# A layer norm in two scalar_tensor_tensor steps, and a down product with its contraction outside

## The chip, the cores and the metric

One core of one Trainium2 chip runs the program. The metric is the device time of one execution in microseconds (us). A core has a matrix engine (TensorE, PE in the rows; PEld are its weight loads), a vector engine (VectorE, DVE), an activation engine (ScalarE, ACT), a general engine (GpSimd, POOL) and SyncE (SP), which here only issues transfers. Each engine runs its own instructions in the order in which the program lists them for it; semaphores order the engines against each other.

## What is computed

One layer of a streaming encoder over 2048 tokens of width 1024. A mixer comes first; its output goes into a layer norm, then into a mixture of 32 experts of which each token uses two, then into a second layer norm and a gated embedding:

```
x   = layer_norm(ALPHA * x + mixer(x), ln1_g, ln1_b)
ffn = moe(x)                       # per token: two experts, weighted by e_w
                                   # expert: (silu(x @ w_eg) * (x @ w_eu)) @ w_ed
x   = layer_norm(ALPHA * x + ffn, ln2_g, ln2_b)
out = x + sigmoid(x @ w_pg + b_pg) * rms_norm(p @ w_pp, ple_g)

def layer_norm(x, g, b):
    mu  = mean(x);  var = mean((x - mu) ** 2)
    return (x - mu) * rsqrt(var + EPS) * g + b
```

## The kernel before

Only the expert phase and the last phase matter here.

**The expert phase** (class Experts, about 900 to 1686 us of the trace) walks a fixed list of items. An item is the gate ("g"), up ("u") or down ("d") product of one block of 128 gathered rows; there are 33 blocks of one expert and 7 pair blocks of two experts, 64 rows each. Weights of single experts come in two units per matrix, are loaded as f32 (eraw), and are split into a high part on ScalarE and a low part on VectorE (ew), so that three matrix products stand for one. Weights of an expert that is seen only in a pair block come as one whole tile of 2 MB and are loaded straight into a weight slot, with no split (L1704). There are seven weight slots, handed on first in, first out: a slot is freed after the item that uses its unit last, and the next unit of the list takes it. The transfer into a reused slot waits, on SyncE's queue, for the last product that reads the old contents.

**A down product** (Block.down) makes 1024 output columns in two halves of 512. For each half it takes one of two PSUM banks with the tag "yo", runs four contraction steps of three products (12 matmuls), and copies the bank to y on ScalarE (L1473). Steps 0 and 1 read the first weight unit (d, 0), steps 2 and 3 the second (d, 1). Between the halves it hands control back to the list (yield), which puts in transposes and weight splits of other items. With this order the first unit is read by the matmuls 1 to 6 and 13 to 18 of 24.

**The last phase** (class Final, 16 tiles of 128 tokens, written t) gathers two expert rows per token (L1810) and the residual (xn), forms the weighted sum (ln, L1826 to L1828, with the row sum as accum_out), calls layer_norm with that sum as total (L901 to L915), transposes the result (tr, L1486, split by L46 on ScalarE and L47 on VectorE), multiplies by w_pg (gate, 48 matmuls, L56 to L58, evicted by L1840), and closes the tile: sigmoid (L1849), product with the embedding (L1850), sum (L1851), store. The embedding's own norm takes a square on ScalarE (L1945), a power and a product with the gain on GpSimd (L1953, L1954); the list places these behind the power L905 of the layer norm three tiles on.

In layer_norm with total given, VectorE makes mean and minus mean (L901, L902), ScalarE squares with accumulation (L903, its elementwise output thrown away into "spare"), VectorE makes the variance (L904), GpSimd takes the power -0.5 (L905), VectorE makes minus mean times that (L906), ScalarE normalises in place (L907), and VectorE multiplies by g and adds b in halves of 512 columns (L914, L915). The scheduler may put instructions of other steps between these. `after(k, ctx, insts)` puts the instructions of a block behind each given instruction, on that instruction's own engine only; RS[t], what layer_norm returns, is used for that.

Buffers: the gathered pair yy has five slots, xn three, the output x2 four from tile 4 on, gt (gate result, and scratch of L1945) two.

Of the kernel before, what the change touches and what calls it, by code (L numbers as in the profile page):

```python
# [12 lines left out]
AF = mybir.ActivationFunctionType  # L13
OP = mybir.AluOpType
# [26 lines left out]
def ptile(k, tag, shape):  # L41
    return k.psp.tile(shape, F32, name=tag, tag=tag, bufs=k.pb[tag])
# [74 lines left out]
def drain(g):  # L117
    for _ in g:
        pass
# [769 lines left out]
def layer_norm(k, p, r, g, b, out, total=None, spare=None, keep=False):  # L889


    nc, v = k.nc, k.nc.vector
    m = p.tile([128, 5], F32, name="lnm", bufs=2)
    if total is None:
        st = p.tile([128, 2, 6], F32, name="lnst", bufs=2)
        for i in range(2):
            v.bn_stats(st[:, i], r[:, 512 * i:512 * i + 512])
        v.bn_aggr(m[:, 0:2], st)
        v.tensor_scalar(m[:, 2:3], m[:, 1:2], EPS, None, OP.add)
    else:  # L900
        v.tensor_scalar(m[:, 0:1], total, 1.0 / D, None, OP.mult)  # L901
        v.tensor_scalar(m[:, 4:5], total, -1.0 / D, None, OP.mult)  # L902
        nc.scalar.activation(spare, r, AF.Square, bias=m[:, 4:5], accum_out=m[:, 1:2])  # L903
        v.tensor_scalar(m[:, 2:3], m[:, 1:2], 1.0 / D, EPS, OP.mult, OP.add)  # L904
    rs = nc.gpsimd.tensor_tensor(m[:, 3:4], m[:, 2:3], k.mhalf[:, 0:1], OP.pow)  # L905
    ms = v.scalar_tensor_tensor(m[:, 4:5], m[:, 0:1], -1.0, m[:, 3:4], OP.mult, OP.mult)  # L906
    no = nc.scalar.activation(r, r, AF.Identity, scale=m[:, 3:4], bias=m[:, 4:5])  # L907
    if total is None:
        rg = out if keep else r
        nc.gpsimd.tensor_tensor(rg, r, g, OP.mult)  # L910
        v.tensor_tensor(out, rg, b, OP.add)
        return rs, no, ms
    for sl in (slice(0, 512), slice(512, 1024)):
        v.tensor_tensor(r[:, sl], r[:, sl], g[:, sl], OP.mult)  # L914
        v.tensor_tensor(out[:, sl], r[:, sl], b[:, sl], OP.add)  # L915
    return rs, no, ms


# [488 lines left out]
class Block:  # L1407
# [54 lines left out]
            self.hT = k.mp.tile([128, 2, 4, 128], F32R, name="hT", tag="hT", bufs=2)  # L1462
            self.ht_done = split(k.nc, k, self.hT[:, 0], self.hT[:, 1], ps)

    def down(self, last=False):
        k = self.k
        y = k.mp.tile([128, 1024], F32, name="y", tag="y", bufs=YB)
        for a in range(2):
            ps = ptile(k, "yo", [128, 512])
            for kc in range(4):  # L1470
                self.mm(ps, self.hT, "d", kc, 512 * a, kc == 0, kc == 3)
            sl = slice(512 * a, 512 * a + 512)
            k.nc.scalar.activation(y[:, sl], ps, AF.Copy)  # L1473
            if last:
                k.nc.scalar.dma_start(self.dst[:, sl], y[:, sl])
            if a == 0:
                yield
        if not last:
            k.nc.scalar.dma_start(self.dst, y)
# [126 lines left out]
class Experts:  # L1606
# [105 lines left out]
    def run(self, then, mid):  # L1712

        k, items, need, blocks = self.k, self.items, self.need, self.blocks
        final = min(i for i, (r, n, b) in enumerate(items) if n == items[-1][1])
        last = {u: i for i, us in enumerate(need) for u in us}
# [22 lines left out]
        g = [blocks[xorder[j]].gather() for j in range(NG)][-1]  # L1739
# [14 lines left out]
        for i, (r, n, b) in enumerate(items):  # L1754
            blk = blocks[n, b]
            if i:
                xstep()
            if i == SORTAT:
                order_tokens(k)
            if i == 2:  # L1760
                ctx.close()
            while not all(u in self.ready for u in need[i]):
                self.wstep()
            if r == "d":
                while blk in pend:
                    hstep()
            m = blk.down(i == len(items) - 1) if r == "d" else blk.up(r)
            next(m)
            hstep()
            self.wstep()  # L1770
            if i == len(items) - 1:
                mid()
            drain(m)
            if r == "u":
                pend.append(blk)
                xlive -= 1
            elif r == "d":
                hlive -= not blk.pair
            for u in need[i]:
                if last[u] == i:  # L1780
                    self.free.append(self.slot[u])
            self.wstep()
            if i >= final:
                then(i - final, blk)
# [3 lines left out]
class Final:  # L1788
# [32 lines left out]
    def ln(self, t, p):  # L1821
        k, nc, v = self.k, self.k.nc, self.k.nc.vector
        y0, y1 = self.Y[t]
        xn = self.XN[t]
        tot = p.tile([128, 1], F32, name="tot", bufs=2)
        nc.scalar.activation(xn, xn, AF.Copy, scale=ALPHA)  # L1826
        v.scalar_tensor_tensor(y0, y0, k.ew[:, 0, t:t + 1], xn, OP.mult, OP.add)  # L1827
        v.scalar_tensor_tensor(y0, y1, k.ew[:, 1, t:t + 1], y0, OP.mult, OP.add, accum_out=tot)  # L1828
        self.X2[t] = y1 if t < INPLACE else p.tile([128, 1024], F32, name="x2", tag="x2", bufs=4)
        self.RS[t] = layer_norm(k, p, y0, k.fin[:, 0], k.fin[:, 1], self.X2[t], tot, y1)  # L1830

    def gate(self, t, amidst=lambda: None):
        k, v, W, XT = self.k, self.k.nc.vector, self.W, self.XT[t]
# [293 lines left out]
```

## Time and profile before

| | us |
|---|---|
| median of 3 runs | 1914.25 (1913.67 to 1916.04) |
| the profiled execution, device time | 1919.0 |
| its span, first to last instruction | 1917.1 |
| TensorE busy in the span | 1837.4 (96%) |
| VectorE busy | 1179.4 (62%) |
| ScalarE busy | 907.8 (47%) |
| GpSimd busy | 318.2 (17%) |

The profile is of one execution. Busy shares are means over stages; a matmul row's duration is longer than its distance to the next one, as matmuls are pipelined. What a stage is worth is read from what its engine waited for there. The clock column of the window rows is the granted TensorE clock as a share of 2.4 GHz; 0.50 stands for 1.2 GHz.

### The profile page before, as it was taken

To read this page: it belongs to the slowest core of one execution; us is meant where nothing else is said; L and a number is where in the kernel's file an instruction comes from. 1 tells how busy PE (TensorE), PEld (TensorE's weight loads), DVE (VectorE), ACT (ScalarE), POOL (GpSimd) and SP (SyncE) were. 2 spreads that over 40 slices of the span, in tenths; PEclk is the share of its full clock that TensorE was granted. 3 is DMA by queue.
4 is the path that set the end of the run, shared out by engine and by line. 5 is a ranking of instruction groups with operands and counts; after the bars stand their busy time and mean duration, and the time that the engine had idled before them with its cause. 6 is when DMAs were issued, how large, how long until landed. Compare 5 with 4: busy or idle time off the path is not lost. (4 is left out here: it accounts for less than half of the span.)

```text
span 1917.1 us, 26807 instructions
## 1 busy us (share of the span) xinstructions
PE 1837.4 (96%) x10016; PEld 1458.7 (76%) x10016; DVE 1179.4 (62%) x2184; ACT 907.8 (47%) x1348; POOL 318.2 (17%) x254
## 2 busy tenths in 40 slices
PE   8999999989999999998999999999999999998898
PEld 6877899989988788876867678575857676776777
DVE  8557665787787444447746356154636256578896
ACT  4343434477777322234645255155536265455442
POOL 0000000033433112211000100000000000137543
PEclk9999999999999999999999999999999999998999
DMA  9698844543455533226988996998799876856632
GB/s 282 200 251 236 216 136 144 190 133 127 149 175 164 181 106 120 100 92 238 384 318 297 352 383 233 327 330 320 274 359 381 327 287 263 334 176 232 224 121 78
DMA packets 232325, 442.86 MB, mean 231 GB/s; under 512 B 46400, under 2 KB 88448, under 8 KB 231296
## 3 DMA queue, kind: packets, MB, share of 16 engines
q1 hardware_dynamic: 205760, 357.07, 54.6%
q0 software_dynamic: 12096, 44.05, 6.4%
q10 hardware_dynamic: 14336, 40.01, 5.3%
q8 instruction: 80, 1.31, 0.3%
q14 instruction: 53, 0.43, 0.1%
HBM read 355.61 MB, written 85.46 MB: 230 GB/s over the span
## 5 line engine op out<-in xcount | busy, mean ns | idle before, releaser
L1371 DVE TENSOR_TENSOR ew<-eraw,ew 128x2048 fp32r<-128x2048 f32 x133 | 302.7, 2291 | 196.3 <-ACT ew L1369 194.9
L1438 PE MATMUL mm<-ew,xt 128*128 128x512 f32 x1584 | 378.0, 394 | 0.0
L1438 PEld LDWEIGHTS mm<-ew,xt 128*128 128x128 f32 x1584 | 295.0, 189 | 65.8 <-issue 5.7
L1369 ACT ACTIVATE ew<-eraw 128x2048 fp32r<-128x2048 f32 x133 | 252.8, 1913 | 78.7 <-PE mm L1438 23.0
L1438 PE MATMUL yo<-ew,hT 128*128 128x512 f32 x792 | 187.8, 393 | 0.1
L56 PE MATMUL mm<-wsp,xsp 128*128 128x512 f32 (+1 forms) x512 | 178.0, 348 | 7.9 <-ACT wsp L46 6.3
L1438 PEld LDWEIGHTS yo<-ew,hT 128*128 128x128 f32 x792 | 147.1, 188 | 37.4 <-issue 5.7
L58 PE MATMUL mm<-wsp,xsp 128*128 128x512 f32 (+1 forms) x512 | 173.7, 339 | 0.5 <-DVE xsp L47 0.5
L57 PE MATMUL mm<-wsp,xsp 128*128 128x512 f32 (+1 forms) x512 | 173.8, 339 | 0.0
L1418 POOL DMA_INDIRECT xg<-x1d,idx x40 | 53.7, 1341 | 703.4 <-PE tr L1486 661.3
L56 PEld LDWEIGHTS mm<-wsp,xsp 128*128 128x128 f32 x512 | 97.2, 190 | 26.3 <-issue 7.2
L56 PE MATMUL mm<-ew,xt 128*128 128x512 f32 (+1 forms) x264 | 106.1, 402 | 2.2 <-DVE yy L1840 2.1
L58 PEld LDWEIGHTS mm<-wsp,xsp 128*128 128x128 f32 x512 | 97.1, 190 | 11.5 <-DVE xsp L47 1.0
L1434 PE MATMUL mm<-ew,xt 128*64 128x512 f32 x320 | 96.6, 633 | 9.7 <-DMA ew<-in_w_eg 9.7
L58 PE MATMUL mm<-ew,xt 128*128 128x512 f32 (+1 forms) x264 | 104.6, 397 | 0.8 <-DVE xt L47 0.8
L57 PEld LDWEIGHTS mm<-wsp,xsp 128*128 128x128 f32 x512 | 97.1, 190 | 10.2 <-DVE wsp L47 0.6
L57 PE MATMUL mm<-ew,xt 128*128 128x512 f32 (+1 forms) x264 | 104.5, 396 | 0.0
L56 PE MATMUL mm<-wsp,mt 128*128 128x512 f32 x256 | 104.3, 408 | 0.0
L58 PE MATMUL mm<-wsp,mt 128*128 128x512 f32 x256 | 102.2, 399 | 0.0
L57 PE MATMUL mm<-wsp,mt 128*128 128x512 f32 x256 | 101.7, 397 | 0.0
L1451 DVE TENSOR_TENSOR h<-h,mm 128x512 f32<-128x512 f32 x40 | 27.4, 685 | 111.2 <-PE mm L1438 90.0
L46 ACT ACTIVATE xt<-tr 128x512 fp32r<-128x512 f32 x98 | 53.6, 591 | 84.6 <-PE tr L1486 84.5
(505 smaller groups left out, 3634.5 us busy)
## 6 DMA issues: line engine op xcount, KB each, us to landing
eraw<-in_w_ed SPq DMA_DIRECT2D x44, 1024.0 KB, 9.2
eraw<-in_w_eu SPq DMA_DIRECT2D x43, 1024.0 KB, 8.3
eraw<-in_w_eg SPq DMA_DIRECT2D x42, 1024.0 KB, 10.2
ew<-in_w_eg SPq DMA_DIRECT2D x10, 2048.0 KB, 10.7
ew<-in_w_eu SPq DMA_DIRECT2D x10, 2048.0 KB, 11.3
ew<-in_w_ed SPq DMA_DIRECT2D x10, 2048.0 KB, 13.0
yb<-y ACTq DMA_DIRECT2D x39, 512.0 KB, 5.6
xraw<-in_xt SPq DMA_DIRECT2D x32, 512.0 KB, 4.6
```

Source lines behind the costliest of these rows:

```text
L46: return (nc.scalar.activation(hi, src, AF.Copy), nc.vector.tensor_tensor(lo, src, hi.bitcast(F32), OP.subtract))
L56: nc.tensor.matmul(ps, lhsT=l[0], rhs=r[0], start=start, stop=False)
L57: nc.tensor.matmul(ps, lhsT=l[0], rhs=r[1], start=False, stop=False)
L58: nc.tensor.matmul(ps, lhsT=l[1], rhs=r[0], start=False, stop=stop)
L1369: h = nc.scalar.activation(w[:, 0], raw, AF.Copy)
L1371: return h, eng.tensor_tensor(w[:, 1], raw, w[:, 0].bitcast(F32), OP.subtract)
L1418: return k.nc.gpsimd.indirect_dma_start(out=self.x, out_offset=None, in_=k.x1d, in_offset=bass.IndirectOffsetOnAxis(ap=self.idx, axis=0))
L1434: mm(ps[sl], lhsT=x[:, kc, sl], rhs=whole_get(u, name, kc, a, a + 512), start=start, stop=stop)
L1438: self.last = mm(ps, lhsT=x[:, l, kc], rhs=w[r], start=start and i == 0, stop=stop and i == 2)
L1451: self.h_done = k.nc.vector.tensor_tensor(self.h, self.h, ps, OP.mult)
```

## The change

Two parts. First, layer_norm with total given: one scalar_tensor_tensor on VectorE writes (r - mean) * g to the output tile, needing the mean but not the power; after the power two scalar_tensor_tensor, one for each half of 512 columns, multiply by the power and add b. L906, L907 and the four products and sums of L914 and L915 are gone from this path. "spare" is now the tile xn instead of y1, since y1 may be the output. RS[t] becomes the power and the two halves (before: the power, the normalisation on ScalarE, and L906). The path without total is as before.

Second, Block.down gets an argument free. It is set for a down item of a single-expert block, not the last item, whose two weight units are both used for the last time: 21 of the 33 by the item list (11 of them follow directly on another down item). Such an item takes both "yo" banks at the start, runs the contraction step outside and the two halves inside, hands control back after step 1, and copies both banks at the end. The unit (d, 0) is then read by the matmuls 1 to 12 only.

```diff
@@ layer_norm, total given
         v.tensor_scalar(m[:, 2:3], m[:, 1:2], 1.0 / D, EPS, OP.mult, OP.add)
+        v.scalar_tensor_tensor(out, r, m[:, 0:1], g, OP.subtract, OP.mult)
     rs = nc.gpsimd.tensor_tensor(m[:, 3:4], m[:, 2:3], k.mhalf[:, 0:1], OP.pow)
+    if total is not None:
+        o = [v.scalar_tensor_tensor(out[:, sl], out[:, sl], m[:, 3:4], b[:, sl], OP.mult, OP.add)
+             for sl in (slice(0, 512), slice(512, 1024))]
+        return rs, o[0], o[1]
     ms = v.scalar_tensor_tensor(m[:, 4:5], m[:, 0:1], -1.0, m[:, 3:4], OP.mult, OP.mult)
     no = nc.scalar.activation(r, r, AF.Identity, scale=m[:, 3:4], bias=m[:, 4:5])
...
-    for sl in (slice(0, 512), slice(512, 1024)):
-        v.tensor_tensor(r[:, sl], r[:, sl], g[:, sl], OP.mult)
-        v.tensor_tensor(out[:, sl], r[:, sl], b[:, sl], OP.add)
     return rs, no, ms
@@ Block.down
+        if free and not self.pair:
+            ps = [ptile(k, "yo", [128, 512]) for a in range(2)]
+            for kc in range(4):
+                for a in range(2):
+                    self.mm(ps[a], self.hT, "d", kc, 512 * a, kc == 0, kc == 3)
+                if kc == 1:
+                    yield
+            for a in range(2):
+                k.nc.scalar.activation(y[:, 512 * a:512 * a + 512], ps[a], AF.Copy)
+            k.nc.scalar.dma_start(self.dst, y)
+            return
@@ Experts.run
-            m = blk.down(i == len(items) - 1) if r == "d" else blk.up(r)
+            end = i == len(items) - 1
+            m = blk.down(end, not end and all(last[u] == i for u in need[i])) if r == "d" else blk.up(r)
@@ Final.ln
-        self.RS[t] = layer_norm(k, p, y0, k.fin[:, 0], k.fin[:, 1], self.X2[t], tot, y1)
+        self.RS[t] = layer_norm(k, p, y0, k.fin[:, 0], k.fin[:, 1], self.X2[t], tot, xn)
```

## Rows read from the trace of the kernel before

**Rows 1.** Windows: length, busy PE, PEld, DVE, ACT, POOL, clock, DMA share, GB/s

```profile
1687.00:1711.00 24.00, 20.30 (x80) 15.99 (x81) 14.55 (x31) 12.55 (x15) 9.68 (x10) 0.86 0.51 175
1711.00:1740.00 29.00, 23.02 (x111) 19.14 (x110) 24.25 (x34) 15.07 (x22) 15.15 (x13) 0.91 0.42 142
1740.00:1800.00 60.00, 51.76 (x219) 42.15 (x218) 52.32 (x80) 28.14 (x39) 39.26 (x31) 0.90 0.73 256
1800.00:1850.00 50.00, 46.09 (x211) 36.65 (x210) 46.05 (x67) 22.93 (x32) 23.60 (x17) 1.00 0.47 157
1850.00:1876.40 26.40, 25.94 (x118) 21.61 (x119) 23.28 (x40) 11.91 (x17) 12.41 (x8) 0.94 0.21 80
```

**Rows 2.** TensorE's waits, 1690 to 1917 us: who waited for whom, total, times, longest

```profile
PE tr L1486 <- DVE x L915: 18.5, 8, 6.0
PE mm L56 <- DVE yy L1840: 2.1, 1, 2.1
PE tr L1486 <- DVE yy L915: 1.6, 1, 1.6
```

**Rows 3.** Timeline of one layer norm, tile 7: start, length, engine, line; idle before it

```profile
1772.03 0.58 POOL L905 TENSOR_TENSOR lnm<-lnm,mhalf 128x1 f32<-128x1 f32 x1
1773.09 2.38 POOL L1954 TENSOR_TENSOR pl<-pl,ew 128x1024 f32<-128x1024 f32 x1
1772.64 2.86 DVE L906 SCALAR_TENSOR_TENSOR lnm<-lnm 128x1 f32<-128x1 f32 x1 [0.91 <-issue]
1775.42 1.27 DVE L1828 SCALAR_TENSOR_TENSOR yy<-yy,ew 128x1024 f32<-128x1024 f32 x1
1775.59 1.24 ACT L907 ACTIVATE yy<-yy,lnm 128x1024 f32<-128x1024 f32 x1 [5.92 <-DVE lnm L906]
1776.62 1.27 DVE L1850 SCALAR_TENSOR_TENSOR gt<-pl,sq,gt 128x1024 f32<-128x1024 f32 x1
1777.82 1.28 DVE L914 TENSOR_TENSOR yy<-yy,ew 128x512 f32<-128x512 f32 x2
1779.03 1.28 DVE L915 TENSOR_TENSOR x<-yy,ew 128x512 f32<-128x512 f32 x2
1779.85 1.08 PE L1486 MATMUL tr<-ident,x 128*128 128x128 f32 x4 [3.38 <-DVE x L915]
```

**Rows 4.** VectorE's waits, 1690 to 1917 us

```profile
DVE lnm L906 <- POOL lnm L905: 11.8, 12, 3.0
```

**Rows 5.** ScalarE's waits, 1690 to 1917 us

```profile
ACT gt L1945 <- DMA out<-gt: 24.2, 4, 6.8
```

**Rows 6.** TensorE's waits in the expert phase, 950 to 1680 us

```profile
PE mm L1434 <- DMA ew<-in_w_eg: 9.7, 4, 3.0
```

**Rows 7.** Timeline around one such wait: TensorE, SyncE's queue (SPq), ScalarE's copies

```profile
1059.69 5.60 PE L1438 MATMUL yo<-ew,hT 128*128 128x512 f32 x24
1063.96 0.37 SPq L1704 DMA_DIRECT2D ew<-in_w_eg  x1
1065.13 5.61 PE L1438 MATMUL mm<-ew,xt 128*128 128x512 f32 x24
1065.33 0.60 ACT L1473 ACTIVATE y<-yo 128x512 f32<-128x512 f32 x1 [2.12 <-PE yo L1438]
1075.62 5.34 PE L1434 MATMUL mm<-ew,xt 128*64 128x512 f32 x14 [3.01 <-DMA ew<-in_w_eg]
```

**Rows 8.** The same 14 matmuls behind two others of the four waits, TensorE

```profile
1212.05 5.34 PE L1434 MATMUL mm<-ew,xt 128*64 128x512 f32 x14 [2.11 <-DMA ew<-in_w_eg]
1508.61 3.65 PE L1434 MATMUL mm<-ew,xt 128*64 128x512 f32 x14 [1.83 <-DMA ew<-in_w_eg]
```

**Rows 9.** Windows: behind the first wait, and ahead of the second

```profile
1074.00:1080.00 6.00, 4.38 (x13) 1.36 (x14) 0.00 (x0) 0.00 (x0) 0.00 (x0) 0.72 1.05 402
1200.00:1202.00 2.00, 2.00 (x11) 1.65 (x10) 0.00 (x0) 0.53 (x1) 0.00 (x0) 1.00 0.00 0
```

**Rows 10.** ScalarE's weight split on the page: count, busy, mean ns, idle before

```profile
L1369 ACT ACTIVATE ew<-eraw 128x2048 fp32r<-128x2048 f32 x133 | 252.8, 1913 | 78.7 <-PE mm L1438 23.0
```

More of the change, by code (lines that the diff above doesn't have):

```diff
@@ L904, in layer_norm @@
         v.tensor_scalar(m[:, 2:3], m[:, 1:2], 1.0 / D, EPS, OP.mult, OP.add)
+        v.scalar_tensor_tensor(out, r, m[:, 0:1], g, OP.subtract, OP.mult)
     rs = nc.gpsimd.tensor_tensor(m[:, 3:4], m[:, 2:3], k.mhalf[:, 0:1], OP.pow)
+    if total is not None:
+        o = [v.scalar_tensor_tensor(out[:, sl], out[:, sl], m[:, 3:4], b[:, sl], OP.mult, OP.add)
+             for sl in (slice(0, 512), slice(512, 1024))]
+        return rs, o[0], o[1]
     ms = v.scalar_tensor_tensor(m[:, 4:5], m[:, 0:1], -1.0, m[:, 3:4], OP.mult, OP.mult)
     no = nc.scalar.activation(r, r, AF.Identity, scale=m[:, 3:4], bias=m[:, 4:5])
[L908 to L912, printed above, removed]
-    for sl in (slice(0, 512), slice(512, 1024)):
-        v.tensor_tensor(r[:, sl], r[:, sl], g[:, sl], OP.mult)
-        v.tensor_tensor(out[:, sl], r[:, sl], b[:, sl], OP.add)
+    rg = out if keep else r
+    nc.gpsimd.tensor_tensor(rg, r, g, OP.mult)
+    v.tensor_tensor(out, rg, b, OP.add)
     return rs, no, ms
@@ L1463, in ht, with down @@
             self.ht_done = split(k.nc, k, self.hT[:, 0], self.hT[:, 1], ps)
-    def down(self, last=False):
+    def down(self, last=False, free=False):
         k = self.k
         y = k.mp.tile([128, 1024], F32, name="y", tag="y", bufs=YB)
+        if free and not self.pair:
[9 more added lines that the diff above has]
+            return
         for a in range(2):
```

## Prediction

> **What bounds the kernel now.** I read the page's busy shares first: TensorE is busy 96% of the span, so time can only come from the places where it waits or runs slowly. The view of TensorE's waits, taken by stretch, names them. In the last phase it waits ten times, 18.5 + 2.1 + 1.6 = 22.2 us, nearly all of it for the second product of the layer norm, L915 [rows 2]. In the expert phase it waits four times for one kind of transfer, 9.7 us, longest 3.0 [rows 6]. The window view adds what the waits alone hide: in the stretches of the last phase where they fall, the mean granted clock is 0.86, 0.91, 0.90 and 0.94, and 1.00 where they hardly occur [rows 1]. Time at a mean clock c in a stretch of length L gives L * (1 - c) of lost work: 24 * 0.14 + 29 * 0.09 + 60 * 0.10 + 26.4 * 0.06 = 3.4 + 2.6 + 6.0 + 1.6 = 13.6 us. So the last phase has at most 22.2 + 13.6 = 35.8 us to give.
>
> What bounds it behind that is VectorE: from 1711 to 1876.4 it is busy 24.25 + 52.32 + 46.05 + 23.28 = 145.9 of 165.4 us [rows 1]. The layer norm is late because its steps queue there, not because its data are.
>
> **The layer norm, along its path.** Tile 7 shows the pattern [rows 3]. The power L905 ends at 1772.6. The tiny L906 then takes 2.86 us and ends at 1775.5, together with GpSimd's 1024-column product L1954 (1773.09 to 1775.47): a VectorE instruction with two SBUF inputs stands still while that one runs. Then ScalarE normalises (1775.59 to 1776.83), meanwhile VectorE has begun L1828 and L1850 (to 1777.82), then come two L914 (to 1779.03) and the first L915; TensorE starts its transposes at 1779.85, 3.38 us late.
>
> After the change the first half is one step of 512 columns away from the power. Two L914 issue in 1777.82 to 1779.03, so 512 columns cost 0.60. It has two SBUF inputs as L906 had, and L1954 still comes right behind the power, so I let it wait as L906 did: 1775.5 + 0.6 = 1776.1, and the transposes could start 3.7 us earlier than 1779.85. This wait of 3.38 is gone, and 1776.1 is what the next limit has to beat.
>
> The new first step, 1024 columns with two inputs, costs VectorE what a scalar_tensor_tensor of that size costs: L1828 starts at 1775.42 and L1850 follows at 1776.62, so 1.20 [rows 3]. Per tile: removed 4 * 0.60 = 2.4 and L906, whose own work is one column; added 1.20 + 2 * 0.60 = 2.4. VectorE's work is unchanged. The first step lies beside ScalarE's square and GpSimd's power, where VectorE otherwise waits for L905 (11.8 us in 12 waits [rows 4]); without that cover it would be 1.2 us of path per tile, still less than is removed. ScalarE loses L907, 1.24 us a tile [rows 3]; it is not the bound, so that counts only as latency.
>
> Buffers: the gathered pair is now last read by the first step and the square, ahead of the power, not by L914, so its slot returns by the 1779.0 - 1772.0 = 7 us of [rows 3] earlier, or a little less, and GpSimd's next gathers can start sooner; a gain I don't price. xn is held longer, till the square ends instead of L1827; its loads on SyncE's queue start later, with pl's loads and the stores of gt queued behind. Its price lies between nothing and a few microseconds in the first tiles; I take nothing, since three slots leave two tiles in between.
>
> The sum for this phase, part by part. The waits around tile 1 (1.6 and 2.1): the first goes, one of the second's two microseconds goes, the clock loss of 3.4 goes with them: 6. The longest, 6.0, tile 4: ScalarE's step and the products go (3.0), the rest of the wait and its clock loss stay: 3. The other seven waits, 18.5 - 6.0 = 12.5, and 6.0 + 1.6 of clock: 20.1 at most. That makes 29. But VectorE cannot give all: of its 19.5 idle us in the stretch some 7 will stay (first tiles, data not there yet), which leaves 12.5; with the 6 of tile 1, ahead of that stretch, 18.5. Between 10 (VectorE stays as loosely packed as now, only tile 1 and two waits gain) and 29 I take **18**, since VectorE's busy share in 1800 to 1850 is already 0.92 at full clock [rows 1]: it can be packed so.
>
> By the Trainium skill, Vector Engine (DVE) Microarchitecture Reference, section "Points that are easy to get wrong", a scalar_tensor_tensor with two SBUF sources that are not bf16 runs at half throughput, which speaks against this change. Here L1850 has two such f32 sources and takes the 1.20 us for 1024 columns that two L914 of 512 take [rows 3]; the trace disagrees, and I give the rule a chance of its own below.
>
> **The down product.** All four waits of [rows 6] are for the second whole tile of a pair block. By the list of items each of these takes the slot of (d, 0) of a single-block down item that the change makes free. [Rows 7] shows the path: 24 matmuls from 1059.69 to 1065.13, 0.227 each; the transfer is issued at 1063.96, just behind the 18th (1063.77); TensorE waits for it until 1075.62. With the contraction outside the slot is free behind the 12th, 6 * 0.227 = 1.36 us earlier. SyncE stands at this transfer, so it goes at once. What it gains depends on whether the transfer engines are free: ahead of the second wait they are idle (0.00) [rows 9], ahead of others they are still at work for part of that time. I take 1.36 twice and 1.0 twice: 4.7 of a possible 5.4.
>
> Behind the waits of 3.01 and 2.11 the next 14 matmuls take 5.34 us, behind the one of 1.83 they take 3.65 [rows 7, 8]; the clock behind the first is 0.72 on the mean of 6 us, part of it at 1.2 GHz [rows 9]. So 1.69 hangs on each of the three longer waits, 5.1 in all. They become about 1.9, 0.8 and 1.6; I take two of three as saved, 3.4, and 0 to 5.1 as bounds.
>
> Against it: both yo banks are taken at the start. In the 11 items that follow another down item directly, the fourth matmul needs the bank that the item before has just filled. There the copy starts 0.20 behind the next item's first matmul and takes 0.60 (1065.33 against 1065.13 [rows 7]), so the bank is free at 0.80; three matmuls cover 0.68. That is 0.1 to 0.2 each, with the semaphore 0.2: 2.2 us. Bounds: 0 (the scheduler puts a transpose between), and, where a 1.9 us weight split of ScalarE (1.913 [rows 10]) stands ahead of the copy, 2.1 each, 23 in all. I take 2.2, since the copy in [rows 7] starts 0.20 behind the matmul: ScalarE stood ready. Behind the free items themselves nobody waits for yo, but y's store goes 0.6 later; three y buffers cover that. Sum: 4.7 + 3.4 - 2.2 = **6**, between -18 and 10.5.
>
> **Sum.** 18 + 6 = 24 off the profiled execution's 1919.0 (span 1917.1), so 1895; that execution is 4.75 above the median of the runs, 1914.25. From the median: **1890 us**. A difference under 0.2%, 3.8 us, is about what a measurement of this kernel cannot tell from none.
>
> **The rivals.**
> 1. VectorE becomes the plain bound. If GpSimd's L1954 blocks the new halves as well as the other two-input steps, and the idle time merely moves from L906 to the new steps, the phase gains only tile 1 and two waits: 6 + 2.5 + 2.3 = 11, with the down part 1 to 6 on top: 1900. For it: 145.9 of 165.4 busy; against it: full clock at 0.92 busy. 0.18.
> 2. Slower: ScalarE's square of the embedding (L1945). Before, RS[t + 1] holds it behind L907 on ScalarE; now RS names only a GpSimd and VectorE instructions, so the scheduler may put it ahead. It waits for the store of gt (four waits, 24.2 us, up to 6.8 [rows 5]), and L903 and L46 would queue behind it. Where half of a 6 us wait comes through to TensorE, with some 2.4 of clock (13.6 over some six long waits), a tile costs 5.4. The gain is eaten at five such tiles; with eight of the twelve it is 43 - 24 = 19 slower: 1933. Against it: ScalarE idles half the phase, and the slots of gt come from the same order as before. 0.08.
> 3. The down part doesn't do what it says, or its new bank waits fall behind weight splits: 11 * 2.1 = 23 against 18 + 8 = 26: 1911. 0.07.
> 4. The half throughput above, as a mechanism here: 2048 more columns' time a tile, 2.4 us on VectorE for 14 tiles, 34 us, against 24: 1924. 0.02.
> 5. The forecast's parts all reach their ceilings: 29 + 10: 1875. 0.05.
>
> **How the numbers follow.** The forecast, 1882 to 1898, has 0.60. Faster: 0.60 + 0.18 + 0.05 = 0.83. Same: 0.07. Slower: 0.08 + 0.02 = 0.10. The range reaches from 1877 over rival 1 and rival 3 to 1911; what is left out is 0.10 above, part of rival 3, and rival 5.
>
> **What would show it.** Right: the waits of tr for the layer norm fall from 20 us to under 6, the clock column is 0.97 or more from 1740 on, the transfer of the pair's second tile is issued behind the 12th matmul, waits for in_w_eg sum to 5 or less. Wrong: L1945's waits for gt's store grow and L46 follows late; VectorE has more blocked two-input steps; TensorE stalls inside free items behind ScalarE's splits. The forecast hangs most on how tightly VectorE can be packed.

## The result, and the profile after

| | before | after |
|---|---|---|
| median of the runs, us | 1915.14 (4 runs, 1913.67 to 1917.68) | 1892.13 (4 runs, 1888.18 to 1894.13) |
| profiled execution, us (span) | 1919.0 (1917.1) | 1894.13 (1892.3) |
| expert phase: first transposes (907.3 and 908.0 us) to the last expert product | 777.7 | 767.6 |
| last phase: last expert product to the end of the span | 232.1 | 216.7 |

The medians differ by 23.0 us. The ratio over all runs is 0.9872 [0.9855, 0.9889], which is 24.5 us of 1915.1 (21.3 to 27.8), where 24 had been forecast (1890). The parts are not as forecast: in these two profiles 15.4 us instead of 18 in the last phase, about 10 instead of 6 in the expert phase.

In the listing after the change, L908 is the pair of new halves, L905 the new first step, L906 the power of the layer norm, L1498 the transposes; L1823 are the gathers of yy, L1813 those of pl, L1839 the scaling of xn, L1853 the gate's eviction, L1866 the scatter of the output, L1958 the embedding's square, L1966 its power, L1967 its product with the gain; in the expert phase L1477 is the copy of a yo bank, L1716 the transfer of a whole tile. L903 and L904 keep their numbers. (The prediction calls L915 a product; it is the addition of b.)

TensorE's waits after the change, one answer for 1690 to 1930 us (first two lines; [rows 2] of before) and one for 950 to 1680 us ([rows 6]): line, who was waited for, total, times, longest.

```profile
PE tr L1498 <- DVE x L908: 12.2, 5, 5.9
PE mm L56 <- DVE yy L1853: 2.3, 1, 2.3
PE mm L1434 <- DMA ew<-in_w_eg: 3.7, 4, 1.3
PE yo L1438 <- ACT y L1477: 0.2, 1, 0.2
```

In the last phase 22.2 us of waits became 14.5; in the expert phase 9.7 became 3.7. Windows of the last phase after the change, columns as in [rows 1]:

```profile
1676.00:1700.00 24.00, 21.39 (x94) 16.83 (x93) 19.84 (x34) 10.72 (x15) 10.03 (x9) 0.93 0.58 187
1700.00:1728.00 28.00, 22.13 (x101) 18.32 (x101) 19.89 (x25) 12.20 (x18) 18.16 (x15) 0.94 0.48 155
1728.00:1780.00 52.00, 46.27 (x202) 37.69 (x202) 46.83 (x63) 20.44 (x30) 34.90 (x30) 0.93 0.78 270
1780.00:1830.00 50.00, 50.00 (x236) 41.87 (x235) 50.00 (x69) 22.62 (x33) 24.67 (x16) 0.98 0.55 179
1830.00:1852.00 22.00, 21.28 (x98) 17.31 (x97) 21.96 (x32) 8.62 (x16) 13.26 (x8) 1.00 0.25 96
```

Length times (1 - clock) over these is 1.7 + 1.7 + 3.6 + 1.0 = 8.0 us against 13.6 before. Waits give 7.7 and the clock 5.6, together 13.3 of the 15.4; the transposes of the last tile indeed stand 13.3 us nearer to the last expert product (188.72 us behind it, 202.02 before). The remaining 2.1 lie behind them. ScalarE's last square of the embedding waits for a store of gt; it starts 14.83 us behind the last transposes before and 12.69 after, and from there to VectorE's last instruction it is 12.4 us in both. ScalarE's timeline, before and after:

```profile
1901.82 1.06 ACT L1945 ACTIVATE gt<-pl 128x1024 f32<-128x1024 f32 x1 [5.69 <-DMA out<-gt]
1877.03 1.06 ACT L1958 ACTIVATE gt<-pl 128x1024 f32<-128x1024 f32 x1 [5.69 <-DMA out<-gt]
```

From 1780 to 1852 VectorE is busy 71.96 of 72 us, but it is not what TensorE waits for there. TensorE is busy 71.28 of these 72 us and waits 0.6; the transposes of the tiles 9 to 12 follow each other at its own pace, 11.77 us, which they also keep in the kernel below that leaves out GpSimd's product. 11.6 of the 12.2 us of waits for the halves lie ahead of 1780.

The largest wait did not change: 5.98 us before, 5.87 after, both for tile 4. Timelines of VectorE, GpSimd and TensorE there before the change (start, length, engine, line):

```profile
1730.39 0.15 DVE L904 TENSOR_SCALAR lnm<-lnm 128x1 f32<-128x1 f32 x1 [0.48 <-ACT yy L903]
1731.46 0.59 POOL L905 TENSOR_TENSOR lnm<-lnm,mhalf 128x1 f32<-128x1 f32 x1
1735.24 1.02 POOL L1810 DMA_INDIRECT yy<-yb,dest  x1 [0.36 <-DMA out<-yy,perm]
1738.65 1.94 PE L1486 MATMUL tr<-ident,x 128*128 128x128 f32 x8 [5.98 <-DVE x L915]
```

and of GpSimd, VectorE and TensorE after it:

```profile
1717.92 1.01 POOL L1866 DMA_INDIRECT out<-yy,perm  x1 [0.30 <-DVE x L905]
1719.24 0.97 POOL L1823 DMA_INDIRECT yy<-yb,dest  x1 [0.30 <-issue]
1720.51 0.94 POOL L1823 DMA_INDIRECT yy<-yb,dest  x1 [0.30 <-issue]
1721.47 0.58 POOL L906 TENSOR_TENSOR lnm<-lnm,mhalf 128x1 f32<-128x1 f32 x1
1722.54 2.34 POOL L1967 TENSOR_TENSOR pl<-pl,ew 128x1024 f32<-128x1024 f32 x1
...
1717.88 0.15 DVE L904 TENSOR_SCALAR lnm<-lnm 128x1 f32<-128x1 f32 x1
1722.09 4.00 DVE L908 SCALAR_TENSOR_TENSOR x<-x,lnm,ew 128x512 f32<-128x512 f32 x2 [2.81 <-POOL lnm L906]
...
1725.58 1.08 PE L1498 MATMUL tr<-ident,x 128*128 128x128 f32 x4 [5.87 <-DVE x L908]
```

After the change the variance L904 is there at 1718.0 and the power starts only at 1721.5, 3.4 us later, behind a scatter and two gathers; before it was 0.9 us, and the gathers stood behind the power. By the program they come earlier since a slot of yy comes free earlier; no run tests that reason. From the power's end to the transposes the path did get shorter, 3.5 us instead of 6.6, and the gathers took 2.5 of these 3.1 us back. The halves take 4.00 us there; the pair at 1701.36, with no product of GpSimd beside it, takes 1.41. Seven pairs of the phase are held up like this, by 0.7 to 2.6 us.

In the expert phase the four waits and the 14 matmuls behind them ([rows 7, 8]), and the first transfer's issue:

```profile
1060.16 5.60 PE L1438 MATMUL yo<-ew,hT 128*128 128x512 f32 x24
1063.08 0.37 SPq L1716 DMA_DIRECT2D ew<-in_w_eg  x1
...
1074.15 3.65 PE L1434 MATMUL mm<-ew,xt 128*64 128x512 f32 x14 [1.06 <-DMA ew<-in_w_eg]
1207.67 3.65 PE L1434 MATMUL mm<-ew,xt 128*64 128x512 f32 x14 [0.80 <-DMA ew<-in_w_eg]
1402.62 3.65 PE L1434 MATMUL mm<-ew,xt 128*64 128x512 f32 x14 [1.30 <-DMA ew<-in_w_eg]
1498.65 3.65 PE L1434 MATMUL mm<-ew,xt 128*64 128x512 f32 x14 [0.50 <-DMA ew<-in_w_eg]
```

The transfer is issued 2.92 us behind the item's first matmul (4.27 before), just behind the 12th matmul, and none of the four groups takes 5.34 us any more.

### The profile page after: what moved, and what is told of

Read it like the earlier page. It is cut to its first block, busy times and chain, and to the rows that moved or that the text cites. A ratio compares the mean times of both kernels' runs of the same rounds, so it can differ in the third digit from the quotient of the medians.

```text
span 1892.3 us, 26759 instructions
## 1 busy us (share of the span) xinstructions
PE 1825.2 (96%) x10016; PEld 1452.2 (77%) x10016; DVE 1178.3 (62%) x2152; ACT 892.7 (47%) x1332; POOL 318.6 (17%) x254
## 4 chain that ended last, share of the span: by engine, by line
PE 49%; DVE 9%; DMA 8%; issue 5%; ACT 3%; POOL 2%; ACTq 0%; SPq 0%; POOLq 0%; DVEq 0%
PE mm L1438 16%; PE yo L1438 8%; PE mm L1434 5%; PE mm L58 4%; PE mm L57 4%; PE mm L56 4%; PE yo L1434 3%; PE tr L1498 2%; DMA ew<-in_w_eg 2%; DVE x L908 1%; DMA eraw<-in_w_eu 1%; PE tr L1457 1%; DVE x L905 1%; DMA ew<-in_w_ed 1%; DVE gt L1863 1%
## 5 line engine op out<-in xcount | busy, mean ns | idle before, releaser
L1369 ACT ACTIVATE ew<-eraw 128x2048 fp32r<-128x2048 f32 x133 | 253.8, 1915 | 92.0 <-PE mm L1438 24.2
L56 PEld LDWEIGHTS mm<-wsp,xsp 128*128 128x128 f32 x512 | 97.1, 190 | 27.8 <-issue 7.2
L56 PE MATMUL mm<-ew,xt 128*128 128x512 f32 (+1 forms) x264 | 104.4, 395 | 2.3 <-DVE yy L1853 2.3
L58 PEld LDWEIGHTS mm<-wsp,xsp 128*128 128x128 f32 x512 | 97.1, 190 | 11.4 <-DVE xsp L47 1.0
L57 PEld LDWEIGHTS mm<-wsp,xsp 128*128 128x128 f32 x512 | 96.9, 189 | 10.1 <-DVE wsp L47 0.4
L58 PE MATMUL mm<-ew,xt 128*128 128x512 f32 (+1 forms) x264 | 103.2, 392 | 0.2 <-DVE xt L47 0.2
L57 PE MATMUL mm<-ew,xt 128*128 128x512 f32 (+1 forms) x264 | 103.3, 391 | 0.0
L1434 PE MATMUL mm<-ew,xt 128*64 128x512 f32 x320 | 91.5, 599 | 3.7 <-DMA ew<-in_w_eg 3.7
## 6 DMA issues: line engine op xcount, KB each, us to landing
eraw<-in_w_eg SPq DMA_DIRECT2D x42, 1024.0 KB, 10.6
```

What stands on the lines that cost most here:

```text
L56: nc.tensor.matmul(ps, lhsT=l[0], rhs=r[0], start=start, stop=False)
L57: nc.tensor.matmul(ps, lhsT=l[0], rhs=r[1], start=False, stop=False)
L58: nc.tensor.matmul(ps, lhsT=l[1], rhs=r[0], start=False, stop=stop)
L1369: h = nc.scalar.activation(w[:, 0], raw, AF.Copy)
L1434: mm(ps[sl], lhsT=x[:, kc, sl], rhs=whole_get(u, name, kc, a, a + 512), start=start, stop=stop)
```

## The experiments

Each kernel is measured by its stages: the two lengths of the table above, read from its own profile. Whole times are less sharp here, since the kernel before itself ran from 1906 to 1924 us on the chips of these runs. The changed kernel was run a second time to see how far a stage repeats.

| kernel | expert phase | last phase | median, us | ratio to before, interval |
|---|---|---|---|---|
| before | 777.7 | 232.1 | 1915.1 | |
| after | 767.6 | 216.7 | 1892.1 | 0.9872 [0.9855, 0.9889] |
| after, once more | 768.1 | 216.3 | 1889.3 | 0.9856 [0.9813, 0.9899] |
| norm only | 776.8 | 217.7 | 1904.9 | 0.9941 [0.992, 0.9962] |
| down only | 769.0 | 231.0 | 1908.8 | 0.9966 [0.9948, 0.9984] |
| no gain product | 768.0 | 204.2 | 1882.1 | 0.9829 [0.9792, 0.9866] |
| gain a tile earlier | 768.0 | 219.8 | 1898.9 | 0.9902 [0.9868, 0.9937] |
| gathers behind the power | 768.6 | 232.8 | 1909.2 | 0.9972 [0.9954, 0.999] |
| square into y1 | 772.0 | 227.2 | 1905.3 | 0.9941 [0.9921, 0.9962] |
| gain in halves | 768.3 | 218.1 | 1895.7 | 0.9905 [0.9884, 0.9926] |
| gain on VectorE | 767.3 | 206.3 | 1882.3 | 0.9829 [0.9812, 0.9846] |
| gain on VectorE, tile 4's gathers late | 767.7 | 209.3 | 1887.4 | 0.985 [0.983, 0.9871] |
| before, gain on VectorE | 772.4 | 216.9 | 1898.6 | 0.9901 [0.9883, 0.9919] |
| square into y1, square first | 767.6 | 222.3 | 1900.9 | 0.992 [0.9894, 0.9946] |

**The changed kernel once more.**

> The changed kernel itself, once more, on the chip of the run beside it. It tells how far stage lengths repeat: the expert phase should again take 767 to 768.5 us from its first transposes to the last product, and the last phase 215.5 to 218; tile 4's transposes should again come 49.5 to 50.5 us behind the last product. If the last phase differs by more than 1.5 us, differences of that size between the other runs say nothing.

It gave 768.1 and 216.3 us, tile 4's transposes 49.3 us behind the last product (50.0 in the first run). Kernels with the same last phase differ by as much as 1.0 us (after and norm only) and 1.1 us (before and down only), so a last phase two microseconds longer says something and one microsecond doesn't. The expert phase spreads more, and the four waits for in_w_eg with the 14 matmuls behind each of them show why. With the old down product three, three and one of the four groups take 5.34 us, and the phase 777.7, 776.8 and 772.4 ("before", "norm only" and "before, gain on VectorE"). With the new one no group does in ten of eleven kernels, and the phase is 767.3 to 769.0; in "square into y1" one does, the waits are 5.8 us, and the phase is 772.0. What decides whether a group takes 5.34 or 3.65 us was not found. TensorE's timelines, two groups of "before, gain on VectorE", one of "norm only" and one of "square into y1":

```profile
1078.13 3.65 PE L1434 MATMUL mm<-ew,xt 128*64 128x512 f32 x14 [2.53 <-DMA ew<-in_w_eg]
1212.88 5.34 PE L1434 MATMUL mm<-ew,xt 128*64 128x512 f32 x14 [2.10 <-DMA ew<-in_w_eg]
1408.11 5.34 PE L1434 MATMUL mm<-ew,xt 128*64 128x512 f32 x14 [2.04 <-DMA ew<-in_w_eg]
1077.06 5.34 PE L1434 MATMUL mm<-ew,xt 128*64 128x512 f32 x14 [2.16 <-DMA ew<-in_w_eg]
```

**Each part alone.**

```diff
 norm only, in Experts.run
-            m = blk.down(end, not end and all(last[u] == i for u in need[i])) if r == "d" else blk.up(r)
+            m = blk.down(end) if r == "d" else blk.up(r)
```

"Down only" is the kernel before with the diff's hunks of Block.down and Experts.run.

> The changed kernel with the down product as it was before; only the layer norm is new. Theory (the two parts add up, each in its own stage): the last expert product ends near 1685 us as in the kernel before (1684.97; 1675.61 after the change), the four waits for in_w_eg sum to 9 to 10 us again, and the last phase is as long as after the change, 216.7 us from the last expert product to the end (232.1 before). The time is about 15 us under the kernel before, near 1900. Rival (the last phase gains only because the faster expert phase leaves its residual and gather transfers another start): the last phase stays over 222 us and the whole gains less than 10.

> The kernel before with the new down product alone. Theory: the last expert product ends near 1675.6 us instead of 1685.0, of which 6 us are shorter waits for in_w_eg (3.7 instead of 9.7) and about 5 us the 14 matmuls behind them (3.65 instead of 5.34 three times), less about 1 us of waits for the yo banks; the last phase stays 232 us long; the time is 9 to 10 us under the kernel before, near 1905. Rival (the down part gives only the 6 us that I forecast, and the rest of what the expert phase gained comes from elsewhere): 1908 to 1909, with the last expert product at 1679.

The stages behave as two separate changes: norm only has the new last phase (217.7) and the old expert phase (776.8), down only the reverse (231.0 and 769.0). In norm only the waits for in_w_eg sum to 8.6 us and three of the four groups of 14 matmuls take 5.34 us; in down only they sum to 4.5 and no group is slow. TensorE's timeline of down only, three of the four:

```profile
1078.31 3.65 PE L1434 MATMUL mm<-ew,xt 128*64 128x512 f32 x14 [1.13 <-DMA ew<-in_w_eg]
1406.22 3.65 PE L1434 MATMUL mm<-ew,xt 128*64 128x512 f32 x14 [1.27 <-DMA ew<-in_w_eg]
1502.70 3.65 PE L1434 MATMUL mm<-ew,xt 128*64 128x512 f32 x14 [0.93 <-DMA ew<-in_w_eg]
```

The down part is worth 8.7 us between these two profiles. The rival value of 6 doesn't fall by that: against the third profile with the old product, 772.4, it is 3.4, and by the ratio of whole times 6.5 (3.1 to 10.0). Norm only is 11.3 (7.3 to 15.3) by its ratio. I had named 1675.6 and 1685.0 us as times for the last product; the runs start their experts at 906.3 and 911.3, so those absolute times were no good measure, and the stage lengths are.

**Without GpSimd's gain product.**

```diff
-                    nc.gpsimd.tensor_tensor(pl, pl, k.fin[:, 3], OP.mult)
```

> The changed kernel without GpSimd's product of the embedding with its gain (pl by fin[:, 3], 128x1024): the output lacks ple_g. In the changed kernel this product stands right behind the layer norm's power on GpSimd, and the pair of new halves on VectorE takes 4.0 us instead of 1.4 wherever the two meet (four tiles at least). Theory (the two engines shut each other out while the product runs, and VectorE stands in a step it has already started): all pairs of halves take 1.4 us, TensorE's waits for the halves fall from 12.2 us to under 6, and the last phase is 5 to 12 us shorter than the 216.7 us after the change. Rival (VectorE is packed by its own work, and the 4.0 us are only work shown in another place): VectorE's idle time grows by what the pairs lose, TensorE's waits stay at 10 us or more, and the last phase shortens by less than 3 us.

The last phase gets 12.5 us shorter still, 204.2. No half takes over 0.75 us, TensorE's waits for the halves fall from 12.2 to 3.6, and the clock in the windows from 1728 to 1852 is 1.00. TensorE's waits from 1690 us on, and tile 4's halves in the timeline:

```profile
PE tr L1498 <- DVE x L908: 3.6, 3, 2.2
```

```profile
1722.57 1.42 DVE L908 SCALAR_TENSOR_TENSOR x<-x,lnm,ew 128x512 f32<-128x512 f32 x2 [2.47 <-POOL lnm L906]
```

So what VectorE lacks after the change is what GpSimd's product takes from it. It lacks it ahead of tile 9, whose transposes already stand 11.7 us nearer to the last product (105.26 against 116.99 us); from there to the last tile only 1.1 us are added.

**The product two tiles on instead of three.**

```diff
-PLA, PLN = 3, 2
+PLA, PLN = 2, 2
```

> The changed kernel with the embedding's product on GpSimd put behind the power of the layer norm two tiles on instead of three (PLA 2 instead of 3), which lets other work stand between a power and a product. Theory (the product right behind the power shuts out the new halves): fewer pairs of halves take 4.0 us (four or more after the change), TensorE's waits for the halves fall below 9 us from 12.2, and the last phase is 2 to 6 us shorter than 216.7. Rival (the product's time is lost to VectorE wherever it stands, since VectorE is busy all the time from 1780 to 1850 us): other two-input steps take the 2.6 us instead, and the last phase stays within 2 us of 216.7.

Two pairs are held up instead of seven, as the theory has it, and yet the phase is 3.1 us longer. The rival is half right: other two-input steps are held up instead. Counted as the time of each VectorE step beyond the mean of its shape where no GpSimd product runs, the last phase has 26.3 us of it after the change and 22.0 here, 10.0 of them now in L1841, 5.8 in L1863 and 4.7 in the halves. And GpSimd's list got worse: its product now waits for the embedding's square twice as long (15.8 after the change). GpSimd's waits from 1690 us on, and VectorE's timeline at two held-up steps:

```profile
POOL pl L1967 <- ACT gt L1958: 31.5, 8, 6.5
```

```profile
1731.03 3.37 DVE L1841 SCALAR_TENSOR_TENSOR yy<-yy,ew 128x1024 f32<-128x1024 f32 x1
1741.68 3.71 DVE L1841 SCALAR_TENSOR_TENSOR yy<-yy,ew 128x1024 f32<-128x1024 f32 x1
```

TensorE then waits 6.5, 4.0 and 3.7 us. The first of these, for tile 4, loses nothing: its transposes stand 49.81 us behind the last product (49.96 after the change). The loss comes behind it, up to tile 7 (93.37 against 89.01), whose power starts 2.7 us behind its variance instead of 0.85. How much of it is GpSimd's list and how much the held-up steps was not separated.

**The product in two halves.**

```diff
-                    nc.gpsimd.tensor_tensor(pl, pl, k.fin[:, 3], OP.mult)
+                    for sl in (slice(0, 512), slice(512, 1024)):
+                        nc.gpsimd.tensor_tensor(pl[:, sl], pl[:, sl], k.fin[:, 3, sl], OP.mult)
```

> The changed kernel with GpSimd's product of the embedding with its gain in two instructions of 512 columns instead of one of 1024. Theory (a two-input step on VectorE waits until the running GpSimd product ends): the first half of the layer norm is shut out for about 1.2 us instead of 2.4, so pairs that took 4.0 us take 2.7 to 3.0 us, or 4.0 again if GpSimd's second half gets in between the two VectorE halves; in the first case TensorE's waits for the halves fall from 12.2 to about 8 and the last phase is 2 to 4 us shorter than 216.7; in the second it is within 1 us.

218.1 us, no gain. Four pairs take 4.1 to 4.2 us, the second of the two outcomes: both GpSimd products run before the waiting VectorE step. Timeline of tile 4, both engines:

```profile
1719.47 2.47 POOL L1968 TENSOR_TENSOR pl<-pl,ew 128x512 f32<-128x512 f32 x2
...
1719.03 4.14 DVE L908 SCALAR_TENSOR_TENSOR x<-x,lnm,ew 128x512 f32<-128x512 f32 x2 [2.82 <-POOL lnm L906]
```

But it is not so everywhere. Where VectorE comes straight from other work, a step does get in between: the half from 1797.90 to 1799.67 ends 0.55 us behind the first product (1797.65 to 1799.12) while the second runs to 1800.83 and takes 1.75 instead of 1.25 us. In all, VectorE is held up for 25.9 us here, against 26.3 with the product in one piece.

**The product on VectorE, and the same in the kernel before.**

```diff
-                    nc.gpsimd.tensor_tensor(pl, pl, k.fin[:, 3], OP.mult)
+                    v.tensor_tensor(pl, pl, k.fin[:, 3], OP.mult)
```

> The changed kernel with the embedding's product with its gain on VectorE (1.2 us of 128x1024) instead of GpSimd (2.35 us). Leaving the product out altogether shortened the last phase from 216.7 to 204.2 us, with no pair of halves over 1.42 us. Theory (GpSimd's product costs more VectorE time by shutting it out than the same work costs on VectorE itself): the halves take 1.4 us everywhere, the last phase is 206 to 213 us, between the two, and the time is 4 to 10 us under that of the changed kernel. Rival (VectorE has no room: it was busy all of 1780 to 1850 us after the change, and 14 products are 17 us): 217 us or more, and the time no better than after the change.

> The kernel before, with old layer norm and old down product, but the embedding's product with its gain on VectorE instead of GpSimd. It tells how much of the layer norm's gain was the old chain itself (ScalarE's step and four products behind the power) and how much only the small two-input step L906 shut out by GpSimd's product for up to 2.3 us. Theory (both count, and they add up): L906 takes 0.14 instead of 2.8 us, and the last phase, 232.1 us in the kernel before and 206.3 with the new layer norm and the product on VectorE, comes to 218 to 226. Rival 1 (the shutting out was all that the old layer norm lost): 206 to 212 us. Rival 2 (VectorE, with 17 us more work, is the bound here): 230 us or more.

On the changed kernel this is the best version of all that compute the whole output: last phase 206.3, median 1882.3, 10 us under the change itself. The groups of VectorE's instructions (count, busy, mean ns, idle before), first of the changed kernel from 1690 us, then of this one from 1700 us:

```profile
L908 DVE SCALAR_TENSOR_TENSOR x<-x,lnm,ew 128x512 f32<-128x512 f32 x24 | 32.5, 1387 | 5.8 <-POOL lnm L906 5.6
L905 DVE SCALAR_TENSOR_TENSOR x<-yy,lnm,ew 128x1024 f32<-128x1024 f32 x12 | 20.9, 1743 | 0.0
```

```profile
L1967 DVE TENSOR_TENSOR pl<-pl,ew 128x1024 f32<-128x1024 f32 x16 | 19.5, 1216 | 0.0
L908 DVE SCALAR_TENSOR_TENSOR x<-x,lnm,ew 128x512 f32<-128x512 f32 x24 | 16.9, 747 | 7.5 <-POOL lnm L906 7.0
L905 DVE SCALAR_TENSOR_TENSOR x<-yy,lnm,ew 128x1024 f32<-128x1024 f32 x12 | 15.3, 1273 | 0.0
```

VectorE gets 19.5 us of work more and 24 * 0.640 + 12 * 0.470 = 21.0 us of being held up less in these two lines, 26.3 over all its steps. So it comes out some 7 us ahead; the rest of what is won is the place, as I read it, since the halves are what TensorE waits for. The shorter list of GpSimd is not the reason: the powers of the tiles 4 to 8 start 11.1 us in sum behind their variances here, and 10.3 after the change.

On the kernel before the same line gives 216.9 instead of 232.1, a little better than the 218 to 226 of the theory. There the victims were L906 and the first products. The groups from 1700 us on, first of the kernel before, then of this one:

```profile
L906 DVE SCALAR_TENSOR_TENSOR lnm<-lnm 128x1 f32<-128x1 f32 x14 | 15.7, 1121 | 12.7 <-POOL lnm L905 11.8 <-issue 0.9
L914 DVE TENSOR_TENSOR yy<-yy,ew 128x512 f32<-128x512 f32 x28 | 22.5, 838 | 1.5 <-ACT yy L907 1.4
```

```profile
L914 DVE TENSOR_TENSOR yy<-yy,ew 128x512 f32<-128x512 f32 x28 | 18.0, 685 | 0.1
L906 DVE SCALAR_TENSOR_TENSOR lnm<-lnm 128x1 f32<-128x1 f32 x14 | 2.2, 160 | 5.6 <-POOL lnm L905 5.2
```

The four kernels make a square for the last phase:

| | gain product on GpSimd | on VectorE |
|---|---|---|
| old layer norm | 232.1 | 216.9 |
| new layer norm | 216.7 | 206.3 |

The new layer norm is worth 15.4 us with the product on GpSimd and 10.6 with it on VectorE; moving the product is worth 15.2 and 10.4. So 10.6 of the change's 15.4 us come without GpSimd's product too, from the shorter chain, and 4.8 only beside it. These 4.8 are not less holding up in sum (27.2 us before, 26.3 after); what they are stays open.

**Tile 4: gathers behind the power.**

```diff
-SEQ = "TPGLNQC"
+SEQ = "TPGNLQC"
...
+                        with ExitStack() as c2:
+                            after(k, c2, [self.RS[t + LEAD][0]])
+                            self.load(t + LEAD + 1)
```

> The changed kernel with the gathers of a later tile (yy) ordered behind the layer norm's power on GpSimd; after the change the power of tile 4 stands behind two of them and one scatter (power at 1721.47 us, its input ready at 1717.95). Theory (GpSimd's queue, not VectorE, makes tile 4's wait of 5.87 us): the two gathers (1.27 and 1.27 us of queue) no longer stand ahead of that power, tile 4's wait falls to 3.0 to 3.6 us, and the last phase is 2 to 4 us shorter than 216.7. Rival (the wait is made by the product behind the power, which shuts out the halves for 2.6 us): tile 4's wait stays over 5 us and the last phase within 1 us of 216.7. Later gathers may make later tiles wait for their rows; if so VectorE's waits for yy's transfers grow from under 2 us to 5 or more.

The path of tile 4 got as short as the theory has it, from the variance's end to the transposes 1716.05 to 1718.53, 2.5 us instead of 7.6; its transposes stand 45.25 us behind the last product instead of 49.96. The wait itself is still 5.58, because TensorE now comes to it earlier: the length of a wait was the wrong thing to forecast, the place of the transposes the right one. But then all later tiles wait for their rows (eleven waits), and the phase is 16.1 us longer. VectorE's waits from 1690 us on:

```profile
DVE yy L1840 <- DMA yy<-yb,dest: 34.7, 11, 4.9
```

With the product on VectorE, and the gathers held back for tile 4 alone (the diff of the last section, and this one only where t + LEAD == INPLACE):

> The changed kernel with the embedding's product on VectorE and, for tile 4 alone, the two gathers of tile 5 behind tile 4's power on GpSimd. With the product on VectorE the last phase was 206.3 us, tile 4's transposes stood 47.31 us behind the last expert product, and the time from tile 4's variance to its transposes was 4.9 us (7.6 after the change). Theory (what is left of tile 4's delay is GpSimd's queue of two gathers, 2.5 us): from variance to transposes 2.4 to 2.8 us, tile 4's transposes at 45 us, the last phase 203 to 206 us if tile 5 doesn't wait for its rows. Rival (as with all gathers moved, tile 5's rows then come late): tile 5's first step waits 2 to 4 us for yy's transfer, and the last phase is 206 us or more.

Variance to transposes 2.4 us, transposes at 43.55 us: the theory of tile 4's delay holds. 2.6 us of it were GpSimd's product and 2.5 the two gathers (7.6, then 4.9 without the product beside it, then 2.4). But tile 5 then waits 3.2 us for its rows, and the phase is 209.3 against 206.3, as the rival has it. Moving the gathers costs more than it gives, in both kernels.

**The square's scratch.**

```diff
-        self.RS[t] = layer_norm(k, p, y0, k.fin[:, 0], k.fin[:, 1], self.X2[t], tot, xn)
+        self.RS[t] = layer_norm(k, p, y0, k.fin[:, 0], k.fin[:, 1], self.X2[t], tot, xn if t < INPLACE else y1)
```

> The changed kernel with ScalarE's square written into the gathered row y1 from tile 4 on (as before the change) instead of into xn. Theory A (I priced the longer hold of xn at nothing; ScalarE's waits for xn's transfer grew from 6.3 us before to 23.2 after, but ScalarE has idle time): those waits fall back to 5 to 10 us and the last phase stays within 1.5 us of 216.7. Theory B (these waits reach VectorE and TensorE): the last phase is 3 to 6 us shorter.

Neither: 10.5 us slower. ScalarE runs its list in order, and with nothing tying xn to the square, the scheduler put the next tile's L1839, which waits for xn's transfer, ahead of the layer norm's own square. ScalarE's and VectorE's timeline at the first of four such waits:

```profile
1739.29 1.06 ACT L1839 ACTIVATE xn<-xn 128x1024 f32<-128x1024 f32 x1 [5.21 <-DMA xn<-x1d]
1740.25 1.14 ACT L903 ACTIVATE yy<-yy,lnm 128x1024 f32<-128x1024 f32 x1
...
1741.51 0.15 DVE L904 TENSOR_SCALAR lnm<-lnm 128x1 f32<-128x1 f32 x1 [3.81 <-ACT yy L903]
```

VectorE's waits in this phase:

```profile
DVE lnm L904 <- ACT yy L903: 11.4, 4, 3.9
```

To see whether that order is all, the order was put back:

```diff
+        k.lnsq = nc.scalar.activation(spare, r, AF.Square, bias=m[:, 4:5], accum_out=m[:, 1:2])
...
+        after(k, ctx, [k.lnsq] if t > INPLACE else []); nc.scalar.activation(xn, xn, AF.Copy, scale=ALPHA); ctx.close()
```

> As the run with the square written into y1 (last phase 227.2 us, 10.5 more than after the change), but with the next tile's scaling of the residual (L1839) ordered behind the layer norm's square (L903) on ScalarE from tile 5 on. With y1 alone the scheduler put L1839, which waits up to 5.2 us for xn's transfer, ahead of L903, and the variance waited 11.4 us for it. Theory (the order on ScalarE, not the slots of yy, made the loss): the waits of the variance for L903 fall under 3 us and the last phase comes back to 215 to 219 us. Rival (the row y1 held until the square ends brings the gathers late): the last phase stays over 223 us.

The waits of L904 fall from 11.4 to 0.8 us and 4.9 us come back, 222.3: between the two. Up to the fourth tile from the end its transposes stand 1 us nearer to the last product than after the change (151.33 against 152.30); the rest is lost behind that, where ScalarE's square of the embedding waits for the store of gt. ScalarE's waits from 1860 us on, this kernel first, then the changed one:

```profile
ACT gt L1958 <- DMA out<-gt: 20.9, 3, 8.8
```

```profile
ACT gt L1958 <- DMA out<-gt: 12.0, 2, 6.3
```

So the loss in the middle was ScalarE's order, 4.9 of the 10.5 us. Whether holding y1 has a part in the loss at the end stays open.

## Why the prediction was right, and where its terms were off

**The layer norm's path, 18 forecast, 15.4 measured.** The mechanism held: tile 7's wait of 3.38 us is gone (its transposes start at 1764.62 with no wait), VectorE's own work is unchanged (unhindered, L905 takes 1.27 us and a half 0.75). But waits also moved: tile 6, which had none, waits 2.80 us, and tile 8 2.69 instead of 2.31. Three terms were mis-sized.

- Tile 4, 3.0 forecast, 0.1 measured. The step that failed is the one on the slot of the gathered pair, "a gain I don't price": I looked only at what an earlier slot gives, not at where its gathers would then stand. They went ahead of tile 4's power on GpSimd, 2.5 us, which ate what the missing ScalarE step and products had given, 3.1 us where 3.0 had been forecast. The kernels that move the gathers show the 2.5, and that these two ways of moving them lose elsewhere.
- Tile 1 and its clock, 6 forecast. By tile 4's transposes 3.7 us are gained (49.96 against 53.68 us behind the last product), of 9 for both terms. One wait of 2.3 us remains there, for the gate's eviction, and the clock of the first two windows is 0.93 and 0.94.
- The other seven waits, 9 after the cap, gave more: 15.4 - 3.7 = 11.7, of which 2.1 lie behind the last transposes, where nothing had been forecast. VectorE's busy share could rise above the 0.92 of [rows 1], to 71.96 of 72 us, but part of that is time in which it is held up, and the cap had no term for that.

**Rival 1** was half of the truth. I had seen GpSimd's product holding up L906 and let the new halves wait for it too, but booked it as delay of one tile's chain. It is VectorE's time: in the busy column it looks like work. Per phase it was 14 * (1121 - 160) ns = 13.5 us in L906 and 28 * (838 - 685) ns = 4.3 in L914 before, and is 21.0 in L908 and L905 after; over all of VectorE's steps it is 27.2 before and 26.3 after. The change moved that loss and did not remove it; that VectorE stood still for so much of its busy time was there to be read. The Trainium skill says this (SBUF — State Buffer, section "Who interferes with whom"): a VectorE instruction with two SBUF inputs contends with a GpSimd instruction that reads SBUF, and one of them stops entirely. The trace agrees, 4.0 against 1.41 us. The same section of the Trainium skill says that issue order, not the shape of an operation, decides who blocks. By the start times in the rows here the halves come 0.45 us ahead of the product (1722.09 and 1722.54) and are held up all the same. Either these starts are not the order of issue, or the rule doesn't hold here; the runs don't tell which.

**Rival 2**, ScalarE's square of the embedding ahead of its turn, did not come: its waits for gt's store are 23.2 us, 24.2 in [rows 5]. The mechanism is real, though: with the scratch in y1 it came with another instruction, L1839. That kernel lost 10.5 us, of which 4.9 came back with the order. I had priced "xn is held longer" at nothing. ScalarE's waits for xn's transfer did grow, from 6.3 us to 23.2; no run shows what that costs by itself, but both kernels without the hold are slower, by 10.5 and 5.6 us.

**The down product, 6 forecast, 8.7 measured alone and 10.1 in the change.** Against the profiled execution of the kernel before, all three terms lay on the cautious side. The waits shrank by 6.0 in the change and 5.2 in down only (4.7 taken, 5.4 called possible); the transfer itself goes 1.35 us earlier, as forecast with 1.36. All three groups behind the long waits run in 3.65 us, 5.1 instead of the 3.4 for two of them. That term is partly luck: another profile with the old product has one slow group and not three, and would have had 1.7 to give. The stalls for the yo banks, forecast with an allowance for the semaphore that no row gives, show as 0.2 to 1.0 us of waits in all runs with the new product, not 2.2, so **rival 3** falls with its 23.

**Rival 4**, half throughput for the new steps, is refuted: L905 with two f32 inputs in SBUF takes 1.27 us for 1024 columns where nothing holds it up, as L1828 did in [rows 3]. **Rival 5** is out: 14.5 us of waits are left.

Of what was to show it: the waits for the halves came to 12.2 us and not under 6 (wrong), the clock is 0.93 until 1780 and 0.98 to 1.00 from there (late), in_w_eg 3.7 (right), the transfer behind the 12th matmul (right). The time is right in part by luck: 2.6 us less than forecast in the last phase and 2.7 to 4.1 more in the expert phase cancel.

## What to carry to other kernels

Where TensorE waits for VectorE, look at the mean length of one group of its instructions against the same shape elsewhere: time in which GpSimd holds it up is shown as busy, and moving a product from GpSimd to a VectorE that is nearly full can still gain (10.4 us here). A buffer that comes free earlier moves the transfers that wait for it, so price their place in the queue of the engine that issues them, not only the slot. And measure a stage by the distance of its events from a fixed point: the length of one wait can stay at 5.6 us while its tile comes 4.7 us sooner.

## What the runs showed of the hardware that I had not expected

Cutting a GpSimd product in two does not free VectorE: at four tiles a pair of halves stands behind both pieces (4.14 us, as long as beside one product of the same size), elsewhere a step gets in between and the second piece takes 1.75 instead of 1.25 us, and the sum of VectorE's held-up time stays (25.9 and 26.3 us). And the start in the row of a held-up instruction does not tell when it gets to work: a pair of halves that begins 0.45 us ahead of the product ends 1.2 us behind it (1722.09 + 4.00 against 1722.54 + 2.34), and in [rows 3] L906, 0.16 us of work where nothing holds it up, begins 0.45 us ahead of L1954 and still ends with it. Moving 16 products of 1024 columns to VectorE cost it 19.5 us and took 40.9 us (2.55 each) off GpSimd.
